# Expert search and dense expert pass: candidates cut from 256 to 50, one-hots on three engines, down projections placed two experts into the next group

## The chip, the cores and the metric

The kernel runs as one program on 1 core of a Trainium2 chip. The metric is device time in microseconds (us). Names of engines: PE is the matrix engine (TensorE; PEld its weight loads), DVE the vector engine, ACT the scalar engine, POOL is GpSimd, SP the engine whose queue issues most DMA transfers. Each engine runs its own instructions strictly in the order in which they stand in its queue.

## The reference, cut to what matters

Two transformer layers (FFN, three attention branches, FFN) are followed by a block with two linear-attention mixers and a product-key expert layer (`_peer`). The change is in that last layer only; all the rest is the same code in both kernels. There are 512 tokens of width 1024, 8 heads, 128 sub-keys per half, 128 x 128 = 16384 experts, each a row of `u_tab` and a row of `v_tab`.

```python
qry = (t @ w_q).reshape(n_tok, 8, 2, 128)
scores = einsum("thpd,hpkd->thpk", qry, sub_keys)          # 128 scores per head and half
s_top, i_top = top_k(scores, 16)
cand = s_top[:, :, 0, :, None] + s_top[:, :, 1, None, :]   # 16 x 16 sums
best, pos = top_k(cand, 16);  idx = take(cand_idx, pos)    # 16 experts per token and head
gate = softmax(best)
act = gelu(einsum("td,thkd->thk", h, u_tab[idx]))
out = einsum("thk,thkd->td", gate * act, v_tab[idx])
```

## The kernel before, in words

**Two ways to one sum.** The first 128 tokens (SPT) take their expert rows by gather: `gathered` issues, on POOL, one indirect DMA for each of 128 (head, k) slots and table (256 in all, plus three steps of run-out), and DVE reduces each (a dot product L1459 for `u`, an accumulation L1466 for `v`). Each call `more(n)` advances that pipeline by n steps, so it is spread over other work; four row buffers (`er`) are in flight. The other 384 tokens (DW) go through ALL 16384 experts densely: in 128 tiles ("experts" in the code, `expert(j)`), activations of 128 experts x 384 tokens are computed on PE, multiplied by a gate matrix that is zero but for the chosen experts, and projected down with `v` in 16 groups of 8 tiles (8 down tiles, m = 0..7, for each group).

**Every matrix product** is `lin`: a 128 x 1024 weight tile is loaded by SP (`raw`, three buffers), split into a high part (`wh`, ACT, L85) and a low part (`wl`, DVE or POOL, L86), and takes 24 matmuls (8 slices x high-high, high-low, low-high). The expert's activation is split the same way into `eh` (ACT, L93) and `el` (DVE, L94).

**Stages of `peer`.** (1) `topk`, first loop, 16 steps (head x half): query product, keys product, and `top16` over 128 scores for four blocks of 128 tokens (five DVE instructions each). (2) `pairs`, for each block of 128 tokens: 256 pair sums on POOL, `top16` over them for 8 heads, then two look-ups (compare on DVE, multiply on POOL over 128 x 2048, reduce on DVE), softmax. The first block's result feeds the gathers; each later block is transposed and *scattered*: for 16 tokens at a time (one tile `stage`, 24 in all) the gate matrix is built by 16 small matmuls of one-hot tiles `lt` (DVE) and `rt` (per token: POOL, DVE or ACT), copied out of PSUM by ACT and written to DRAM (`gate_d`). (3) the dense groups: groups 4 to 15 compute their experts; the activations of groups 0 to 3 (EARLY) were made during stage 2 by `ahead` and are read back from DRAM (`act_d`) at the end.

**What sets the order.** The program is written in one stream; a scheduler assigns each instruction to its engine's queue by that order and by estimated readiness. What stands earlier in the text generally stands earlier in each queue. In the dense part, each group's 8 down tiles come in the text directly behind its 8 experts (L1526 on).

Of the kernel before, what the change touches and what calls it, by code (L numbers as in the profile page):

```python
# [29 lines left out]
TB = 16  # L30
SPT = 128
DW = 512 - SPT
ROUND = 1.5 * 2.0 ** 23
EARLY = 4
# [10 lines left out]
class K:  # L45
# [1423 lines left out]
    def peer(self):  # L1469
# [6 lines left out]
        with tc.tile_pool(name="peer", bufs=1) as mp:  # L1476
            self.mp = mp
            io = mp.tile([128, 144], F, name="io")
            nc.sync.dma_start(io, a["iota"])
            sel = [mp.tile([128, DW], F, name=f"sel{i}") for i in range(5)]  # L1480
# [5 lines left out]
            def more(n):  # L1486
                for _ in range(n):
                    next(rows, None)
# [11 lines left out]
            def ahead(n):  # L1500
                for _, j in zip(range(n), early):
                    nc.sync.dma_start(ad[j], expert(j))

            with tc.tile_pool(name="topk", bufs=1) as tp:
                self.topk(tp, hh, hl, rr, io, sel, gd, ahead, more)
            with tc.tile_pool(name="exp", bufs=1) as ep:
                groups = list(range(EARLY, 16)) + list(range(EARLY))
                for g in groups:
                    wh, wl = [], []
                    last = g == groups[-1]  # L1510
                    for e in range(8):
                        j = g * 8 + e
                        if e == 0:
                            gt = ep.tile([128, DW // TB, 8, TB], F, name="gt", bufs=2)
                            nc.sync.dma_start(gt, gd[:, :, j:j + 8, :])
                        if g < EARLY:
                            act = mp.tile([128, DW], F, name="act", bufs=4)
                            nc.sync.dma_start(act, ad[j])
                        else:
                            act = expert(j)  # L1520
                        av = act.rearrange("p (b t) -> p b t", t=TB)
                        nc.gpsimd.tensor_mul(av, av, gt[:, :, e, :])  # L1522
                        h = ep.tile([128, DW], FR, name="eh", bufs=11)
                        q = ep.tile([128, DW], FR, name="el", bufs=11)
                        self.hilo(act, h, q)
                        wh.append(h)  # L1526
                        wl.append(q)
                        more(0 if last else 1)
                    if g == groups[-2]:
                        more(256)  # L1530
                    for m in range(8):
                        if last and m % 4 == 0:
                            pt = self.bank("pt")
                            for i in range(4):
                                k = m + i
                                nc.tensor.transpose(pt[:, i * 128:i * 128 + 128], self.acc[:, k * 128:k * 128 + 128], self.idn)
                            for i in range(4):
                                x = self.x[m + i][:, 0:SPT]
                                nc.vector.tensor_add(x, pt[:, i * 128:i * 128 + 128], x)
                        ps = self.lin(a["pv"][g, m], 8, wh, wl, cols=slice(0, DW))  # L1540
                        x = self.x[m][:, dn]
                        nc.vector.tensor_add(x, ps[:, 0:DW], x)
                        more(1 if g >= EARLY else 0)
                        if last:
                            self.square(m, m == 7)
                            t = self.xtile()
                            nc.scalar.activation(t, self.x[m], AF.Copy, scale=self.vec[:, 64 + m:65 + m])
                            self.x[m] = t

    def topk(self, sp, hh, hl, rr, io, sel, gd, ahead, more):  # L1550
# [3 lines left out]
        sif = sp.tile([128, 4, 8, 2, 16], F, name="sif")  # L1554
        with tc.tile_pool(name="topk1", bufs=1) as mp:
# [6 lines left out]
            for j in range(16):  # L1562
                ps = self.lin(a["pwq"][j], 8, hh, hl, nc.gpsimd)
                x = mp.tile([128, 512], F, name="qt", bufs=2)
                nc.vector.tensor_mul(x, ps, rr)
                ps = self.bank("sc")
                for t in range(4):
                    c = slice(t * 128, t * 128 + 128)
                    nc.tensor.matmul(ps[:, c], x[:, c], keys[j // 4][:, j % 4], start=True, stop=True)
                s = mp.tile([128, 512], F, name="sc", bufs=2)  # L1570
                nc.scalar.copy(s, ps)
                for t in range(4):
                    w = mp.tile([128, 128], F, name="scr", bufs=2)
                    self.top16(sv[:, t, j // 2, j % 2], si[:, t, j // 2, j % 2], s[:, t * 128:t * 128 + 128], w)
            nc.vector.tensor_copy(sif, si)
        with tc.tile_pool(name="topk2", bufs=1) as mp:
            self.pairs(mp, sv, sif, io, sel, gd, ahead, more)

    def pairs(self, mp, sv, sif, io, sel, gd, ahead, more):
        nc = self.nc  # L1580
        b3, b4 = [128, 8, 16], [128, 8, 16, 16]
        for t in range(4):
            ahead((6, 4, 4, 4)[t])
            s0 = t * 128 - SPT
            cand = mp.tile(b4, F, name="cand", tag="big", bufs=2)
            nc.gpsimd.tensor_tensor(cand, sv[:, t, :, 0].unsqueeze(3).to_broadcast(b4), sv[:, t, :, 1].unsqueeze(2).to_broadcast(b4), op=OP.add)
            best = mp.tile(b3, F, name="best", bufs=1)
            pos = mp.tile(b3, U32, name="pos", bufs=1)
            for h in range(8):
                w = mp.tile([128, 256], F, name="scr2", bufs=2)  # L1590
                self.top16(best[:, h], pos[:, h], cand[:, h].rearrange("p a b -> p (a b)"), w)
            res = [mp.tile(b3, F, name=f"res{i}", bufs=1) for i in range(3)]

            pf = mp.tile(b3, F, name="pf", bufs=1)
            pa = mp.tile(b3, F, name="pa", bufs=1)
            nc.vector.tensor_copy(pf, pos)
            nc.vector.tensor_scalar(pa, pf, -7.5, 0.0625, op0=OP.add, op1=OP.mult)
            nc.vector.tensor_scalar(pa, pa, ROUND, ROUND, op0=OP.add, op1=OP.subtract)
            nc.vector.scalar_tensor_tensor(pf, pa, -16.0, pf, op0=OP.mult, op1=OP.add)
            for x, pf in enumerate((pa, pf)):  # L1600
                e = mp.tile(b4, F, name="eq", tag="big", bufs=2)
                nc.vector.tensor_tensor(e, pf.unsqueeze(3).to_broadcast(b4), io[:, 128:144].unsqueeze(1).unsqueeze(1).to_broadcast(b4), op=OP.is_equal)
                nc.gpsimd.tensor_tensor(e, e, sif[:, t, :, x].unsqueeze(2).to_broadcast(b4), op=OP.mult)
                nc.vector.tensor_reduce(res[x], e, axis=AX.X, op=OP.add)
            g = res[2]
            nc.vector.tensor_tensor(g, best, best[:, :, 0:1].to_broadcast(b3), op=OP.subtract)
            nc.scalar.activation(g, g, AF.Exp)
            z = mp.tile([128, 8], F, name="gz", bufs=1)
            nc.vector.tensor_reduce(z, g, axis=AX.X, op=OP.add)
            nc.vector.reciprocal(z, z)  # L1610
            nc.vector.tensor_tensor(g, g, z.unsqueeze(2).to_broadcast(b3), op=OP.mult)
            if s0 < 0:
                nc.vector.scalar_tensor_tensor(res[0], res[0], 128.0, res[1], op0=OP.mult, op1=OP.add)
                nc.vector.tensor_copy(self.eidx, res[0].rearrange("p h k -> p (h k)"))
                nc.vector.tensor_copy(self.egate, g.rearrange("p h k -> p (h k)"))
                continue
            pt = self.bank("pt")
            for i in range(3):
                nc.tensor.transpose(pt[:, i * 128:i * 128 + 128], res[i].rearrange("p h k -> p (h k)"), self.idn)
            for i in range(3):  # L1620
                nc.vector.tensor_copy(sel[i][:, s0:s0 + 128], pt[:, i * 128:i * 128 + 128])
            nc.vector.tensor_scalar(sel[3][:, s0:s0 + 128], pt[:, 128:256], -1.0, None, op0=OP.mult)
            nc.vector.tensor_scalar(sel[4][:, s0:s0 + 128], pt[:, 256:384], -1.0, None, op0=OP.mult)
            for tb in range(s0 // TB, (s0 + 128) // TB):
                st = mp.tile([128, 128, TB], F, name="stage", bufs=2)
                for t4 in range(TB // 4):
                    ps = self.bank("g")
# [193 lines left out]
```

## Time and profile before

| | |
|---|---|
| three runs | 4918.76, 4922.48, 4921.11 us; median 4921.11 |
| profiled execution | 4921.75 us, span of its instructions 4920.0 us, mean granted clock 0.965 |
| busy over the span | PE 93%, PEld 80%, DVE 65%, ACT 39%, POOL 25% |
| peer layer | from about 3300 us to the end |

The profile is of one execution. Matmuls overlap in the pipeline, so the time of a PE row is longer than its distance to the next row; distances of starts are what counts. "Idle before <- X" says what the engine waited for.

### The profile page before, as it was taken

To read this page: it belongs to the slowest core of one execution; us is meant where nothing else is said; L and a number is where in the kernel's file an instruction comes from. 1 tells how busy PE (TensorE), PEld (TensorE's weight loads), DVE (VectorE), ACT (ScalarE), POOL (GpSimd) and SP (SyncE) were. 2 spreads that over 40 slices of the span, in tenths; PEclk is the share of its full clock that TensorE was granted. 3 is DMA by queue.
4 is the path that set the end of the run, shared out by engine and by line. 5 is a ranking of instruction groups with operands and counts; after the bars stand their busy time and mean duration, and the time that the engine had idled before them with its cause. 6 is when DMAs were issued, how large, how long until landed. Compare 5 with 4: busy or idle time off the path is not lost. (4 is left out here: it accounts for less than half of the span.)

```text
span 4920.0 us, 63316 instructions
## 1 busy us (share of the span) xinstructions
PE 4557.3 (93%) x23070; PEld 3912.1 (80%) x23070; DVE 3198.9 (65%) x6028; ACT 1935.8 (39%) x3343; POOL 1213.8 (25%) x1061
## 2 busy tenths in 40 slices
PE   9999999999999999999999998879677899999987
PEld 7887777788888878777888787767666899999986
DVE  4447877654454478787544578778776666666676
ACT  3235565532232256655322332332466333333322
POOL 0001012200000011132100102322688434434454
PEclk9999999999999999999999998989899999999998
DMA  3234333522333343235333332232354777777785
GB/s 129 94 109 129 93 88 84 176 94 92 98 98 94 102 134 96 79 96 164 98 97 97 110 127 79 73 105 82 124 174 169 248 256 245 240 252 247 238 296 190
DMA packets 276311, 688.30 MB, mean 140 GB/s; under 512 B 32192, under 2 KB 92256, under 8 KB 272928
## 3 DMA queue, kind: packets, MB, share of 16 engines
q1 hardware_dynamic: 239136, 550.02, 35.6%
q0 software_dynamic: 36864, 134.23, 8.2%
q8 instruction: 183, 3.00, 0.2%
q14 instruction: 128, 1.05, 0.1%
HBM read 593.04 MB, written 68.04 MB: 134 GB/s over the span
## 5 line engine op out<-in xcount | busy, mean ns | idle before, releaser
L85 ACT CAST wh<-raw 128x1024 fp32r<-128x1024 f32 (+3 forms) x773 | 766.5, 993 | 1773.7 <-PE bk L107 1130.0
L107 PE MATMUL bk<-hh,wh 128*128 128x512 f32 (+1 forms) x3016 | 1138.3, 377 | 27.4 <-ACT hh L231 9.4
L107 PE MATMUL bk<-hh,wl 128*128 128x512 f32 (+1 forms) x3016 | 1133.6, 376 | 21.8 <-DVE wl L86 20.0
L107 PE MATMUL bk<-hl,wh 128*128 128x512 f32 (+1 forms) x3016 | 1132.8, 376 | 0.5 <-DVE hl L232 0.5
L86 DVE TENSOR_TENSOR wl<-raw,wh 128x1024 fp32r<-128x1024 f32 (+3 forms) x693 | 830.1, 1199 | 159.1 <-ACT wh L85 150.4
L107 PEld LDWEIGHTS bk<-hh,wh 128*128 128x128 f32 x3016 | 574.6, 191 | 109.6 <-issue 16.9
L107 PEld LDWEIGHTS bk<-hh,wl 128*128 128x128 f32 x3016 | 573.9, 190 | 102.8 <-DVE wl L86 23.1
L107 PEld LDWEIGHTS bk<-hl,wh 128*128 128x128 f32 x3016 | 574.4, 190 | 79.4 <-issue 2.7
L107 PE MATMUL bk<-eh,wh 128*128 128x384 f32 x1024 | 366.5, 359 | 71.6 <-ACT eh L93 51.9
L197 POOL TENSOR_TENSOR sq<-sq,sqt 128x512 f32<-128x512 f32 x62 | 104.0, 1677 | 1203.5 <-ACT sqt L193 1184.3
L107 PE MATMUL bk<-el,wh 128*128 128x384 f32 x1024 | 365.9, 358 | 12.2 <-DVE el L94 11.0
L107 PE MATMUL bk<-eh,wl 128*128 128x384 f32 x1024 | 360.2, 354 | 10.6 <-DVE wl L86 10.5
L86 POOL TENSOR_TENSOR wl<-raw,wh 128x1024 fp32r<-128x1024 f32 (+2 forms) x80 | 185.3, 2317 | 587.7 <-ACT wh L85 468.3
L107 PE MATMUL bk<-gh,wh 128*128 128x512 f32 x704 | 274.0, 389 | 0.0
L107 PE MATMUL bk<-gh,wl 128*128 128x512 f32 x704 | 273.9, 389 | 0.0
L107 PE MATMUL bk<-gl,wh 128*128 128x512 f32 x704 | 273.9, 389 | 0.0
L107 PEld LDWEIGHTS bk<-eh,wh 128*128 128x128 f32 x1024 | 207.1, 202 | 82.3 <-ACT eh L93 59.9
L1522 POOL TENSOR_TENSOR act<-act,gt 128x384 f32<-128x384 f32 x128 | 173.5, 1361 | 303.1 <-ACT act L1495 190.0
L256 DVE TENSOR_TENSOR t<-bk,rr 128x512 f32<-128x512 f32 x88 | 60.8, 691 | 269.2 <-PE bk L107 269.2
L107 PEld LDWEIGHTS bk<-el,wh 128*128 128x128 f32 x1024 | 206.3, 201 | 22.2 <-DVE el L94 22.0
L107 PEld LDWEIGHTS bk<-eh,wl 128*128 128x128 f32 x1024 | 206.0, 201 | 13.9 <-DVE wl L86 13.9
L265 DVE SCALAR_TENSOR_TENSOR x<-bk,x 128x512 f32<-128x512 f32 x96 | 66.4, 691 | 231.6 <-PE bk L107 231.6
(703 smaller groups left out, 8827.0 us busy)
## 6 DMA issues: line engine op xcount, KB each, us to landing
raw<-in_wi SPq DMA_DIRECT2D x176, 512.0 KB
raw<-in_pu SPq DMA_DIRECT2D x128, 512.0 KB
raw<-in_pv SPq DMA_DIRECT2D x128, 512.0 KB
raw<-in_wo SPq DMA_DIRECT2D x64, 448.0 KB
raw<-in_mg SPq DMA_DIRECT2D x48, 512.0 KB
gate_d<-stage SPq DMA_DIRECT2D x24, 1024.0 KB
gt<-gate_d SPq DMA_DIRECT2D x16, 1536.0 KB
raw<-in_wo SPq DMA_DIRECT2D x32, 512.0 KB
```

What stands on the lines that cost most here:

```text
L85: self.nc.scalar.copy(wh[:, :n], raw[:, :n])
L86: (eng or self.nc.vector).tensor_sub(wl[:, :n], raw[:, :n], wh[:, :n].bitcast(F))
L107: self.nc.tensor.matmul(ps, x[:, c], y[k], start=(n == 0), stop=(n == 3 * kk - 1))
L197: nc.gpsimd.tensor_add(self.sq, self.sq, t)
L256: nc.vector.tensor_mul(t2, pb, rr)
L265: nc.vector.scalar_tensor_tensor(self.x[m], ps, 0.5, self.x[m], op0=OP.mult, op1=OP.add)
L1522: nc.gpsimd.tensor_mul(av, av, gt[:, :, e, :])
```

## The change

- The candidate sums are cut to those pairs of ranks (a, b) that can be among the best 16, (a+1)(b+1) <= 16: 50 in place of 256 (`RANKS`, `FIRST`, `NC2`). They are built by seven POOL instructions per head for all four token blocks; block 0 is searched inside stage 1. Positions are turned into sub-keys by a comparison with the first position of each row (`found`).
- Generators run the search for block t+1 between the 16-token tiles of the scatter of block t (`run`, `pairs`, `fill`, `scatter`).
- `lt` is built for 8 tokens at once. Of 16 tokens' `rt`, ACT makes 6, POOL 5, DVE 5; before it was ACT 4, DVE 4, POOL 8.
- In stage 1 the query is copied by ACT, and the normalisation is applied by ACT as a scale per token.
- EARLY is 5, and ten of those 40 tiles are computed inside stage 1 (j >= 6), six around the first two searches (their `wl` on POOL), 24 in the scatter (one per tile of 16 tokens). The early groups are put between the others: 5, 6, 0, 7, 8, 1, ... 14, 4, 15.
- The 8 down tiles of a group stand behind the second expert of the next group (`e == 1`), the last group's at the end. `el` is made by POOL in place of DVE. The gather steps are spread anew: 12 in the fill, two per scatter tile, 9 or 8 per group of experts and of down tiles, all before the last down.

```diff
-EARLY = 4
+EARLY = 5
...
+        groups = list(range(EARLY, 16))
+        for i in range(EARLY):
+            groups.insert(3 * i + 2, i)
...
                 h = ep.tile([128, DW], FR, name="eh", bufs=11)
                 q = ep.tile([128, DW], FR, name="el", bufs=11)
-                        self.hilo(act, h, q)
+                nc.scalar.copy(h, act)
+                nc.gpsimd.tensor_sub(q, act, h.bitcast(F))
...
+                more(0 if g < EARLY else 1 + (e == 0))
+                if e == 1 and before:
+                    down(*before, False)
+            before = (g, wh, wl)
+        more(256)
+        down(*before, True)
...
-                nc.vector.tensor_mul(x, ps, rr)
+                nc.scalar.copy(x, ps)
...
+                if j % 2:
+                    for r0, r1 in ((0, 1), (1, 2), (2, 3), (3, 4), (4, 5), (5, 8), (8, 16)):
+                        n, w = r1 - r0, RANKS[r0]
+                        nc.gpsimd.tensor_tensor(cand[:, :, h, FIRST[r0]:FIRST[r1]] ...
+                    pair(0, h)
+                if j >= 6:
+                    ahead(1, nc.gpsimd)
...
+            run(pairs(0), fill(3, 0))
+            run(pairs(1), fill(3, 4))
+            for t in range(1, 4):
+                run(self.scatter(mp, t, io, sel, gd, ahead, more), *[pairs(t + 1)] if t < 3 else [])
...
+        e = mp.tile(b4, F, name="eq", tag="big", bufs=1)
+        nc.vector.tensor_tensor(e, pf..., io[:, 144:160]..., op=OP.is_ge)
+        nc.gpsimd.tensor_tensor(e, e, row..., op=OP.mult)
+        yield
...
+                    if v % 3 == 0:
+                        nc.scalar.activation(rt[:, u], io[:, 0:128], AF.Square, scale=-1.0, bias=sel[1][:, i:i + 1])
+                        nc.scalar.activation(rt[:, u], rt[:, u], AF.Relu, scale=sel[3][:, i:i + 1], bias=g)
+                    else:
+                        (nc.gpsimd if v % 3 == 1 else nc.vector).tensor_scalar(rt[:, u], ...
```

**DVE, search and scatter.** Before, the two look-ups of token block 2 (`eq`, L1602 and L1604) with nothing of a scatter between them:

```order
L1599 SCALAR_TENSOR_TENSOR pf<-pa,pf 128x128
L1602 TENSOR_TENSOR eq<-pa,io 128x2048
L1602 TENSOR_TENSOR eq<-pf,io 128x2048
L1604 TENSOR_REDUCE res_31414<-eq 128x128
L1604 TENSOR_REDUCE res_31415<-eq 128x128
L1609 TENSOR_REDUCE gz<-res_31416 128x8
L1493 TENSOR_TENSOR t_31535<-bk,rr 128x384
```

After, the same search's comparison (L1659) among the one-hots `lt` and `rt` of block 1:

```order
L1708 TENSOR_TENSOR lt<-io,sel_28986 128x1024
L1721 TENSOR_SCALAR rt<-io,sel_28987,sel_28988 128x128 x2
L1657 CAST pf<-pos 128x128
L91 TENSOR_TENSOR wl<-raw,wh 128x1024
L1721 TENSOR_SCALAR rt<-io,sel_28987,sel_28988 128x128
L1659 TENSOR_TENSOR eq<-pf,io 128x2048
L1708 TENSOR_TENSOR lt<-io,sel_28986 128x1024
L1498 TENSOR_TENSOR t_31456<-bk,rr 128x384
```

The look-ups no longer stand alone; DVE has one-hots of another block before and behind each.

**DVE, dense part.** Before, one expert of a group (`t` takes its sum from PSUM, `el` needs ACT's `eh`, L1459 is a gather step), and the next expert's `t`:

```order
L1493 TENSOR_TENSOR t_34958<-bk,rr 128x384
L86 TENSOR_TENSOR wl<-raw,wh 128x1024
L94 TENSOR_TENSOR el<-act,eh 128x384
L1459 ISA er,dot<-er,ht 128x1024
L1459 ISA dot 128x1
L1493 TENSOR_TENSOR t_35001<-bk,rr 128x384
```

After, the place between two groups (`x` adds a down tile's sum): a down tile of an early group, two experts of the next group, then the down tiles go on with the following group's.

```order
L1533 TENSOR_TENSOR x<-bk,x 128x384
L1471 SCALAR_TENSOR_TENSOR acc<-er,ew,acc 128x1024
L91 TENSOR_TENSOR wl<-raw,wh 128x1024
L1498 TENSOR_TENSOR t_36463<-bk,rr 128x384
L1471 SCALAR_TENSOR_TENSOR acc<-er,ew,acc 128x1024
L91 TENSOR_TENSOR wl<-raw,wh 128x1024
L1471 SCALAR_TENSOR_TENSOR acc<-er,ew,acc 128x1024
L1498 TENSOR_TENSOR t_36509<-bk,rr 128x384
L1471 SCALAR_TENSOR_TENSOR acc<-er,ew,acc 128x1024
```

`el` is gone from this queue, so that nothing in it waits for `eh`; experts and down tiles alternate in runs of 2, 6 or 8.

**POOL, dense part.** Before, experts at a group's end and the gathers of its down tiles:

```order
L1522 TENSOR_TENSOR act<-act,gt 128x384
L1452 DMA er<-in_pur,eidx 128x1024
L1452 DMA er<-in_pvr,eidx 128x1024 x4
L1452 DMA er<-in_pur,eidx 128x1024 x4
L1522 TENSOR_TENSOR act<-act,gt 128x384
```

After, the end of group 6, which the early group 0 follows:

```order
L1555 TENSOR_TENSOR act<-act,gt 128x384
L1559 TENSOR_TENSOR el<-act,eh 128x384
L1457 DMA er<-in_pur,eidx 128x1024
L1555 TENSOR_TENSOR act<-act,gt 128x384 x3
L1559 TENSOR_TENSOR el<-act,eh 128x384 x2
L1457 DMA er<-in_pur,eidx 128x1024 x2
L1559 TENSOR_TENSOR el<-act,eh 128x384
```

Each expert has a second POOL operation, `el`, that waits for ACT's `eh`; at this place the gate products of group 0's first two tiles stand ahead of the `el` of group 6's last one.

## Rows read from the trace of the kernel before

**Rows 1.** Stretches: us, busy of PE, PEld, DVE, ACT, POOL, clock, DMA share, GB/s

```profile
3423.00:3519.00 96.00, 66.99 (x325) 63.03 (x324) 80.96 (x219) 27.62 (x36) 35.61 (x10) 0.84 0.29 88
3519.00:3596.00 77.00, 59.88 (x368) 51.56 (x366) 56.69 (x140) 59.81 (x106) 75.60 (x70) 0.98 0.55 190
3596.00:3623.00 27.00, 17.61 (x74) 15.99 (x74) 20.26 (x35) 8.74 (x13) 16.19 (x6) 0.81 0.35 127
3818.00:3860.00 42.00, 34.26 (x176) 32.62 (x175) 29.98 (x33) 14.31 (x24) 18.79 (x17) 0.88 0.86 270
3860.00:4612.00 752.00, 701.31 (x3833) 688.65 (x3832) 501.07 (x664) 246.60 (x341) 306.90 (x240) 0.96 0.75 246
4690.00:4903.00 213.00, 182.44 (x945) 173.32 (x943) 160.88 (x196) 61.14 (x88) 109.76 (x84) 0.90 0.74 251
```

**Rows 2.** Dense part, DVE in order of time, 4268 to 4312 us

```profile
4272.16 0.56 DVE L1493 TENSOR_TENSOR t<-bk,rr 128x384 f32<-128x384 f32 x1 [1.35 <-PE bk L107]
4275.75 0.56 DVE L94 TENSOR_TENSOR el<-act,eh 128x384 fp32r<-128x384 f32 x1 [1.45 <-ACT eh L93]
...
4306.93 0.55 DVE L1493 TENSOR_TENSOR t<-bk,rr 128x384 f32<-128x384 f32 x1
```

**Rows 3.** PE in order of time at the start of a group's down tiles

```profile
4303.18 0.34 PE L107 MATMUL bk<-eh,wh 128*128 128x384 f32 x1
4303.35 0.34 PE L107 MATMUL bk<-el,wh 128*128 128x384 f32 x1
...
4306.15 0.34 PE L107 MATMUL bk<-eh,wl 128*128 128x384 f32 x1
4310.06 0.69 PE L107 MATMUL bk<-eh,wh 128*128 128x384 f32 x1 [3.57 <-ACT eh L93]
...
4311.45 0.53 PE L107 MATMUL bk<-eh,wh 128*128 128x384 f32 x1
4311.77 0.53 PE L107 MATMUL bk<-el,wh 128*128 128x384 f32 x1
```

**Rows 4.** ACT's copies of the scores, one per step of stage 1

```profile
L1571 ACT COPY sc<-sc x16: 575/587/588, 3315.1 to 3422.9; 128x512 f32<-128x512 f32 x16
```

**Rows 5.** Groups by line, stage 1 (3315 to 3423): busy, mean ns, idle before

```profile
L1418 DVE MAX8 sv<-scr 128x8 f32<-128x128 f32 x60 | 16.8, 280 | 0.5
L1569 PE MATMUL sc<-keys,qt 128*128 128x128 f32 x120 | 17.0, 285 | 8.8 <-DVE qt L1565 7.2 <-issue 1.7
```

**Rows 6.** The same view, scatter of all three blocks (3519 to 3818)

```profile
L1641 POOL TENSOR_SCALAR rt<-io,sel,sel 128x128 f32<-128x128 f32 x191 | 211.6, 1115 | 9.4 <-DVE sel L1622 8.2 <-issue 0.3
L1644 ACT COPY stage<-g 128x512 f32<-128x512 f32 x96 | 101.0, 1052 | 56.2 <-PE g L1643 56.1
L1639 ACT ACTIVATE rt<-rt,sel,sel 128x128 f32<-128x128 f32 x96 | 46.8, 490 | 2.1
L1638 ACT ACTIVATE rt<-io,sel 128x128 f32<-128x128 f32 x94 | 36.7, 393 | 0.0
L1641 DVE TENSOR_SCALAR rt<-io,sel,sel 128x128 f32<-128x128 f32 x95 | 32.8, 345 | 0.0
L86 DVE TENSOR_TENSOR wl<-raw,wh 128x1024 fp32r<-128x1024 f32 x22 | 27.2, 1243 | 0.0
L1603 POOL TENSOR_TENSOR eq<-eq,sif 128x2048 f32<-128x2048 f32 x4 | 22.1, 5542 | 25.0 <-DVE eq L1602 25.0
L85 ACT CAST wh<-raw 128x1024 fp32r<-128x1024 f32 x21 | 22.0, 1045 | 34.2 <-PE bk L107 24.8 <-DVE gz L1610 9.4
L1459 DVE CUSTOM_DVE_ANT_0 er<-er,ht 128x1024 f32<-128x1024 f32 x13 | 17.0, 1307 | 3.7 <-DMA er<-in_pur,eidx 3.7
L1604 DVE TENSOR_REDUCE res<-eq 128x128 f32<-128x2048 f32 x4 | 9.1, 2286 | 13.3 <-POOL eq L1603 13.3
```

**Rows 7.** The same view, ten dense groups (3860 to 4612)

```profile
L1522 POOL TENSOR_TENSOR act<-act,gt 128x384 f32<-128x384 f32 x80 | 109.0, 1362 | 231.2 <-ACT act L1495 170.3 <-issue 60.8
L1452 POOL DMA_INDIRECT er<-in_pur,eidx x80 | 106.3, 1329 | 110.0 <-DVE acc L1466 84.0 <-DMA raw<-in_pu 19.9 <-issue 4.1
```

More of the change, by code (lines that the diff above doesn't have):

```diff
@@ L32 @@
 DW = 512 - SPT
+RANKS = [16 // (a + 1) for a in range(16)]
+FIRST = [sum(RANKS[:a]) for a in range(17)]
+NC2 = FIRST[16]
 ROUND = 1.5 * 2.0 ** 23
-EARLY = 4
+EARLY = 5
 EPS = 1e-6
@@ L1477, in peer @@
             self.mp = mp
-            io = mp.tile([128, 144], F, name="io")
+            io = mp.tile([128, 176], F, name="io")
             nc.sync.dma_start(io, a["iota"])
-            sel = [mp.tile([128, DW], F, name=f"sel{i}") for i in range(5)]
+            sel = [mp.tile([128, DW], F, name=f"sel{i}") for i in range(4)]
             ht = self.by_token(rc)
@@ L1498, in peer, with ahead @@
             early = iter(range(EARLY * 8))
-            def ahead(n):
+            def ahead(n, eng=None):
                 for _, j in zip(range(n), early):
-                    nc.sync.dma_start(ad[j], expert(j))
+                    nc.sync.dma_start(ad[j], expert(j, eng))
             with tc.tile_pool(name="topk", bufs=1) as tp:
-                self.topk(tp, hh, hl, rr, io, sel, gd, ahead, more)
+                self.topk(tp, hh, hl, rc, io, sel, gd, ahead, more)
             with tc.tile_pool(name="exp", bufs=1) as ep:
[L1507 to L1524, printed above, removed]
-                        self.hilo(act, h, q)
[L1526 to L1548, printed above, removed]
@@ L1552, in topk @@
+    def topk(self, sp, hh, hl, rc, io, sel, gd, ahead, more):
         nc, tc, a = self.nc, self.tc, self.a
@@ new lines, in topk, with run, pairs, fill @@
+        with tc.tile_pool(name="topk2", bufs=1) as mp:
+            def run(*gens):
+                gens = list(gens)
+                while gens:
+                    for g in list(gens):
+                        if next(g, gens) is gens:
+                            gens.remove(g)
+            def pairs(t):
+                if t:
+                    for h in range(8):
+                        pair(t, h)
+                        if h % 2:
+                            yield
+                for _ in self.found(mp, t, best[:, t], pos[:, t], sif[:, t, :, 1], row[:, t], io, sel):
+                    yield
+            def fill(n, m):
+                for _ in range(n):
+                    ahead(1, nc.gpsimd)
+                    more(m)
+                    yield
+            run(pairs(0), fill(3, 0))
+            run(pairs(1), fill(3, 4))
+            for t in range(1, 4):
+                run(self.scatter(mp, t, io, sel, gd, ahead, more), *[pairs(t + 1)] if t < 3 else [])
@@ L1648, in pairs @@
-        ahead(32)
+        res = [mp.tile(b3, F, name=f"res{i}", bufs=1) for i in range(3)]
+        pf = mp.tile(b3, F, name="pf", bufs=1)
+        pa = mp.tile(b3, F, name="pa", bufs=1)
+        nc.vector.tensor_copy(pf, pos)
+        e = mp.tile(b4, F, name="eq", tag="big", bufs=1)
+        nc.vector.tensor_tensor(e, pf.unsqueeze(3).to_broadcast(b4), io[:, 144:160].unsqueeze(1).unsqueeze(1).to_broadcast(b4), op=OP.is_ge)
+        nc.gpsimd.tensor_tensor(e, e, row.unsqueeze(2).to_broadcast(b4), op=OP.mult)
```

192 lines of the change are left out of this document (123 added, 69 removed).

## The prediction

> **What bounds the kernel now.** I read the profile in this order: the busy shares by stretch, then the order in time of DVE and PE where PE falls idle in the dense part, then the groups by line of the three stages. The stretches [rows 1] are the first search (3423 to 3519), eight of the scatter's 24 blocks (3519 to 3596), a gap between two token blocks (3596 to 3623), and the dense part, which begins at 3818. PE is the engine to feed: the tail is 17 us, all else up to 4903 is products. One product of 24 matmuls costs PE 24 x 0.173 = 4.16 us, from the distance of starts where it runs undisturbed (4303.18 to 4303.35) [rows 3].
>
> In the dense part 94 experts are left at 3818 (128 less 32 early ones less the two that the order has done by then) and 128 down tiles: 222 x 4.16 = 923.5 us, but it takes 4903 - 3818 = 1085. So 161 us are lost. Ten groups in the middle take 752 us for 160 products, which need 666: 8.6 us lost for each. The 42 us at the start hold about seven products (29), 13 lost; the 213 us at the end, with four early groups in a row, hold 39 (162), 51 lost [rows 1].
>
> The loss stands at a group's turn. DVE's queue holds, per expert, `t`, `wl`, `el` and a gather step, and `el` waits for ACT's `eh` (1.45 us idle); seven experts take 4306.93 - 4272.16 = 34.8 us, 4.97 each [rows 2]. That is 0.81 more than PE needs, so DVE is 5.6 us behind at the eighth, and the down tiles, which need that expert at once, leave PE idle for 3.57 us at one wait, after which starts are 0.32 apart instead of 0.17, the lower of the clock's two levels (1.2 for 2.4 GHz) [rows 3].
>
> In the scatter POOL is busy 75.6 of 77 us: 9.6 per block of 16 tokens, and in the gaps 16.2 of 27 while PE stands at 17.6 [rows 1]. The stage takes 299 us: 24 x 9.6 = 231, and 68 for two searches with no scatter beside them. POOL's multiply in a look-up (5.5 us) waits 25 us in four for DVE's comparison, and DVE's reduce 13 for POOL [rows 6].
>
> **The change, step by step.** The sum is against the profiled execution, 4921.75 us (0.6 above the median of the runs), whose span is 4920.0.
>
> *Stage 1.* A step takes (3422.9 - 3315.1)/15 = 7.19 us [rows 4], of which PE is idle 8.8/15 = 0.6 for the query that DVE copies [rows 5]; ACT's copy removes about half. Six steps at 6.9 and ten with an expert (6.6 + 4.16 = 10.8) give 149: last scores at about 3464 instead of 3423. Ten products for 41 us: neither gain nor loss. DVE has, per step, four `top16` (1.2 each: five instructions of about 0.25, MAX8 being 0.28 for 128 [rows 5]), half of a block-0 pair search and `t`: about 6, hidden under 10.8. Without that cover the ten steps would each cost a few tenths.
>
> *First search.* The 96 us [rows 1] shrink to what follows the last score. The look-ups pass serially through one buffer: compare about 2.3, multiply 5.54, reduce 2.29 [rows 6], 1 of hand-over: 11.1, four times is 44. Finishing scans 9; eight gathers that POOL's new order puts ahead of the third multiply, at 1.33 [rows 7], about 11; transposes 5. The first block starts near 3464 + 70 = 3534 (bounds 3515, if the searches overlap, and 3550). Six early experts, 25 us of PE, lie under these 70; PE waits for the rest of them.
>
> *Scatter block.* From rows 6 and 7: POOL 5 x 1.115, two gather issues of 1.33 and an eighth of two multiplies: 9.6. ACT 6 x (0.393 + 0.490) + 4 x 1.052 + 1.045 for `wh`: 10.6. DVE `lt` 2 x 1.24 (no row has this form; `wl` is as wide; 0.6 if it ran at twice that rate, 2.5 at half), 5 x 0.345, `wl` 1.24, `t` 0.55 [rows 2], two dot products of 1.31: 8.6, and for the next search (2 x 2.3 + 2 x 2.29 + 8 scans of 0.9 + 2)/8 = 2.3: 10.9. PE has an expert and 16 small products, about 7, and waits. Three engines at nearly one length must meet in each block, so below 9.6 is excluded; if they take turns it is 13 or more. I take 11.0 for sixteen blocks, near the longest engine as POOL's 9.6 was in before, and 10.5 for the last eight, without search: 260 us (bounds 238 and 312). The scatter ends near 3794, with 40 experts done instead of 34.
>
> *Dense part.* 88 experts and 128 down tiles remain: 216 x 4.16 = 898.6. Without `el`, DVE has per expert 4.97 - 1.45 - 0.56 = 2.96: no longer late. POOL has `act` and `el`, 1.36 each (the nearest row is `act`, same shape), about 0.6 of waiting for `eh`, and one issue of 1.33 [rows 7]: 4.65, which is 0.5 above PE's 4.16, so now POOL falls behind, by 4 us over eight experts. At the turns: after groups 5, 7, 9, 11, 13 two experts (8.3 us) cover it, 1 us lost each: 5. The early groups 0 to 4 have no experts; two of the next group stand before their down tiles, while POOL makes 16 products and `el`, 22 us, and gathers in 41: 4 each, 20. Groups 6, 8, 10, 12, 14 are followed by an early group, so nothing of PE's stands between their eighth expert and their down tiles, and the order shows POOL's products for the early group ahead of the eighth `el`: 9 each, as now: 45. The last group 6, the start 12 (13 now). Losses 88 instead of 161 (bounds 48 and 160). Spreading the gathers puts their end ahead of the last down tile; the order shows no gather step behind it, so the tail stays 17.
>
> Sum: 3794 + 898.6 + 88 + 17 = 4797.6 of span, and 1.75 around it: **4799 us**, 122 less. Of these, 24 are the earlier end of the scatter, 25 the six experts more, 73 the turns.
>
> **The shared port.** DVE is busy 501 of 752 us in the dense part [rows 1], mostly with operations on two tiles, and POOL's `act` still averages 1.36 [rows 7] against 0.56 for DVE's `el` of the same shape [rows 2]. The Trainium skill (SBUF — State Buffer, "Who interferes with whom") says that a DVE instruction with two SBUF inputs and a GpSimd instruction that reads SBUF contend for a port pair that is held exclusively. The trace of before neither shows such a wait nor excludes that 1.36 holds one. By that rule 256 POOL operations where 128 stood would meet it; what it would cost is the slower rival.
>
> **The rivals.**
> - *B, scatter blocks of 13 us.* ACT, DVE and POOL are each near 10 to 11 and hand tiles to one another through few buffers. For: POOL already waits for DVE's `eq` [rows 6]. Against: before, POOL kept 75.6 of 77 us [rows 1]. 24 x 13 = 312, 52 more: 4851.
> - *C, the turns stall as before, behind POOL instead of DVE; the two experts between do not help.* Eleven turns at 8.6, five early at 11, start 12: 160 lost instead of 88: 4871. For: 4.65 is over 4.16. Against: 8.3 us of cover exceeds the lag of 4. In part this is the change not doing what it says, since six of sixteen groups' down tiles have no expert between anyway.
> - *D, everything overlaps better.* Blocks of 10 (20 less) and 48 lost (40 less): 4740.
> - *A, POOL sets the pace of the dense part.* It has 256 products and subtractions and 199 gather issues: 128 x (2.72 + 0.6) + 199 x 1.33 = 690 us against 987 forecast. If each of the 455 is held 1.0 us behind DVE's operations, 1145: end 3794 + 1145 + 17, 4958 us, slower. It binds from 0.65 us per operation, and is slower than before from (1109 - 690)/455 = 0.92. Against: DVE was as busy and 1.36 came out [rows 1, 7].
>
> **How the numbers follow.** Forecast 0.46, B 0.18, C 0.12, D 0.12, A 0.08, and B with C together 0.04: 4923, no change. Less than 0.2%, 10 us, cannot be told from none by such runs. Faster is all but A and the last: 0.88; same 0.04; slower 0.08. The likeliest case's own range is 4770 to 4830. For 8 in 10 it must take in B and C and most of D, and leaves out A, B with C, and half of D: 4745 to 4890.
>
> **What the profile after would show.** The first block of the scatter near 3534; blocks 10.5 to 11 apart, with ACT and DVE as busy as POOL; the end near 3794. In the dense part no wait of DVE for `eh`, POOL's `el` at about 1.36, PE's idle before down tiles of 1 us where two experts stand between, and about 9 with a low clock after groups 6, 8, 10, 12, 14. Gathers that end before the last down tile. It is wrong if `el` on POOL takes well over 2 us, if blocks are beyond 12, or if PE waits for gate or weight loads in the early groups, which now stand between the others.

## The result, and the profile after

The changed kernel takes 4833.0 us (median of four runs, 4826.6 to 4839.2) against 4921.8 for the kernel before: a ratio of 0.9821, interval [0.9803, 0.9838]. That is 89 us (1.8%) less where the prediction had 122; it lies in the stated range and 3 us above the likeliest case's own (4770 to 4830). The profiled execution is the fastest of the four, 4826.6 us with a span of 4824.8.

The same view as [rows 1], now in five stretches: stage 1, what follows its last score, the scatter with searches beside it, the scatter of the last token block, the dense part.

```profile
3307.00:3446.00 139.00, 139.00 (x721) 121.50 (x720) 93.31 (x617) 59.43 (x121) 67.12 (x73) 1.00 0.35 104
3446.00:3529.00 83.00, 51.25 (x235) 47.91 (x234) 73.27 (x176) 22.25 (x36) 48.66 (x29) 0.79 0.48 154
3529.00:3712.00 183.00, 137.00 (x779) 124.23 (x778) 145.82 (x258) 142.86 (x281) 166.55 (x110) 0.86 0.64 218
3729.00:3816.00 87.00, 72.16 (x441) 66.75 (x440) 64.61 (x96) 71.89 (x140) 80.06 (x55) 0.95 0.73 251
3815.00:4807.00 992.00, 938.76 (x5191) 930.11 (x5190) 709.90 (x755) 333.28 (x468) 615.08 (x459) 0.97 0.74 251
```

Stage 1 is all PE, at full clock. POOL is still the busiest engine of the scatter (166.6 of 183, 80.1 of 87), and in the dense part its share has grown by half: 615 of 992 us (62%), where it was 307 of 752 (41%) [rows 1]. Against the working of the prediction:

| step | forecast | measured |
|---|---|---|
| last score | 3464 | 3445 |
| first block of the scatter | 3534, 70 later | 3529, 84 later |
| length of the scatter, to PE's last product of it | 260 | 285 |
| dense part, 216 products of 4.16 | 898.6 | 898.6 |
| lost there | 88 | 94 |
| behind the last down tile | 17 | 17.4 |
| span | 4797.6 | 4824.8 |

Against the kernel before, the scatter ends about 3 us earlier (3814.5; its last product was at 3817.1), six more experts are done by then (25 us), and the dense part loses 94 us instead of 161 (67): together 95, and the spans differ by 95.2.

**The scatter.** Groups by line over it, as in [rows 6] (busy, mean ns, idle before):

```profile
L1721 POOL TENSOR_SCALAR rt<-io,sel,sel 128x128 f32<-128x128 f32 x119 | 182.6, 1539 | 16.1 <-issue 5.7 <-ACT wh L90 5.0 <-ACT rt L1719 1.8
L1725 ACT COPY stage<-g 128x512 f32<-128x512 f32 x96 | 100.5, 1053 | 52.3 <-PE g L1724 51.4 <-issue 0.4
L1708 DVE TENSOR_TENSOR lt<-io,sel 128x1024 f32<-128x1024 f32 x47 | 58.1, 1236 | 0.0
L1721 DVE TENSOR_SCALAR rt<-io,sel,sel 128x128 f32<-128x128 f32 x118 | 46.1, 420 | 55.0 <-POOL rt L1721 23.5 <-issue 18.3 <-ACT rt L1718 4.0
L1668 DVE TENSOR_TENSOR res<-res,gz 128x128 f32<-128x128 f32 x2 | 0.7, 352 | 0.0
```

`lt` costs 1.24 us, as estimated, but POOL's `rt` 1.54 where 1.115 was taken from [rows 6]. Five of them are 2.1 us more per block. Blocks follow each other at 12.1 us while a search runs and at 11.2 without one (forecast 11.0 and 10.5); the step to the last token block, 18 us, is in neither mean. With it the first sixteen blocks take 199 us and the last eight 86, where 176 and 84 were forecast.

What stretches them is easiest to see in the second search, where operations stand alone. POOL in order of time:

```profile
3460.03 4.58 POOL L1660 TENSOR_TENSOR eq<-eq,row 128x2048 f32<-128x2048 f32 x1 [5.56 <-DVE eq L1659]
...
3515.80 4.51 POOL L1678 TENSOR_TENSOR eq<-eq,sif 128x2048 f32<-128x2048 f32 x1 [5.89 <-DVE eq L1677]
```

and DVE at the same two moments:

```profile
3460.49 4.27 DVE L1668 TENSOR_TENSOR res<-res,gz 128x128 f32<-128x128 f32 x1
...
3517.01 4.38 DVE L91 TENSOR_TENSOR wl<-raw,wh 128x1024 fp32r<-128x1024 f32 x1
```

A product of two small tiles that takes 0.35 us in the scatter's mean row takes 4.27, and `wl` 4.38 instead of 1.24: each ends only behind POOL's long multiply, `res` 0.15 us after it and `wl` 1.08. In the scatter it goes the other way too. Sorted by what ran beside them ("on two tiles" means that both inputs are tiles in SBUF), POOL's 118 `rt` of the scatter take 0.80 us where DVE runs nothing on two tiles, and about 2.0 where it does for half of their time or more; before the change the same classes had 0.78 and 1.41, beside `lt` tiles half as wide. The Trainium skill (SBUF — State Buffer, "Who interferes with whom") states this: a DVE instruction with two inputs in SBUF and a GpSimd instruction that reads SBUF cannot run together, and the second waits out the first. The traces agree, by the times just given.

**The dense part.** What PE lost at its turns, from the distances of PE's starts in order of time: all over 0.173 us in the gaps, and the starts at the lower clock (about 0.31 apart) behind them. Turns with two experts between are called covered below, those of the second line straight.

| turn | forecast | measured |
|---|---|---|
| five with two experts between (behind 5, 7, 9, 11, 13) | 5 | 34 |
| five straight behind the eighth expert (6, 8, 10, 12, 14) | 45 | 32 |
| five of early groups | 20 | 6 |
| last group, start, and the remainder | 6, 12, 0 | 5, 8, 9 |

So the sum came out near (88 and 94), but not by its terms. The covered turns should have cost 1 us each, and they cost most. PE at such a turn, in the second down tile of group 11:

```profile
4424.30 0.34 PE L112 MATMUL bk<-el,wh 128*128 128x384 f32 x1
4428.98 0.69 PE L112 MATMUL bk<-eh,wl 128*128 128x384 f32 x1 [4.34 <-DVE wl L91]
4429.47 0.52 PE L112 MATMUL bk<-eh,wh 128*128 128x384 f32 x1
4429.78 0.52 PE L112 MATMUL bk<-el,wh 128*128 128x384 f32 x1
```

Not the group's `eh` or `el` is late, as in [rows 3], but the weight's low part. DVE in order of time says why:

```profile
4418.61 0.55 DVE L1498 TENSOR_TENSOR t<-bk,rr 128x384 f32<-128x384 f32 x1
4426.56 1.23 DVE L1464 CUSTOM_DVE_ANT_0 er<-er,ht 128x1024 f32<-128x1024 f32 x1 [7.40 <-DMA er<-in_pur,eidx]
4427.71 0.08 DVE L1464 DVE_READ_ACCUMULATOR2_ANT dot<- 128x1 f32 x1
4427.71 1.22 DVE L91 TENSOR_TENSOR wl<-raw,wh 128x1024 fp32r<-128x1024 f32 x1
```

DVE stood 7.4 us at a gather step, with `wl` behind it. The row it waited for goes into the buffer that this step freed on DVE:

```profile
4403.84 1.96 DVE L1471 SCALAR_TENSOR_TENSOR acc<-er,ew,acc 128x1024 f32<-128x1024 f32 x1
```

which ends at 4405.80; POOL asked for the row 9.4 us later, at 4415.24, behind the products of two experts:

```profile
4408.43 1.72 POOL L1559 TENSOR_TENSOR el<-act,eh 128x384 fp32r<-128x384 f32 x1 [0.63 <-ACT eh L1558]
4410.30 1.79 POOL L1457 DMA_INDIRECT er<-in_pur,eidx  x1
4412.10 1.02 POOL L1555 TENSOR_TENSOR act<-act,gt 128x384 f32<-128x384 f32 x1
4413.75 1.34 POOL L1559 TENSOR_TENSOR el<-act,eh 128x384 fp32r<-128x384 f32 x1 [0.63 <-ACT eh L1558]
4415.24 0.98 POOL L1457 DMA_INDIRECT er<-in_pur,eidx  x1
```

The n-th issue on POOL belongs to the n-th step on DVE and uses the buffer of step n - 4. Over the dense part the issue comes 6.9 us (median) after its buffer is free; before the change it came 0.3 after. So POOL's lag, which the prediction saw, reaches PE by way of the gathers and DVE.

The late issue is not all of it. The rows then took 11.3 us, and at the same time 1.5 MB of gates are loaded for the next group, issued at 4413.15. At all five covered turns the row that DVE waits for was asked for 8 to 11 us after its buffer was free and 2 us behind such a load, and came 9.4 to 11.9 us after it was asked for; at the step of 4718.1, with no load near, a waited-for row came after 5.4. What the load adds by itself was not tried.

DVE did not become lighter either. Its groups over the dense part (the same three with `el` back on DVE stand in that experiment):

```profile
L91 DVE TENSOR_TENSOR wl<-raw,wh 128x1024 fp32r<-128x1024 f32 x209 | 296.2, 1417 | 31.0 <-ACT wh L90 30.8
L1471 DVE SCALAR_TENSOR_TENSOR acc<-er,ew,acc 128x1024 f32<-128x1024 f32 x100 | 156.3, 1563 | 22.8 <-DMA er<-in_pvr,eidx 22.7
L1464 DVE CUSTOM_DVE_ANT_0 er<-er,ht 128x1024 f32<-128x1024 f32 x93 | 143.9, 1548 | 38.5 <-DMA er<-in_pur,eidx 38.4
```

### The profile page after: what moved, and what is told of

It reads as the page before. It is cut to its first block, busy times and chain, and to the rows that moved or that the text cites. A ratio compares the mean times of both kernels' runs of the same rounds, so it can differ in the third digit from the quotient of the medians.

```text
span 4824.8 us, 63302 instructions
## 1 busy us (share of the span) xinstructions
PE 4528.9 (94%) x23070; PEld 3914.1 (81%) x23070; DVE 3171.7 (66%) x5836; ACT 1976.6 (41%) x3515; POOL 1412.6 (29%) x1185
## 5 line engine op out<-in xcount | busy, mean ns | idle before, releaser
L91 DVE TENSOR_TENSOR wl<-raw,wh 128x1024 fp32r<-128x1024 f32 (+3 forms) x677 | 842.7, 1246 | 144.3 <-ACT wh L90 137.7
L91 POOL TENSOR_TENSOR wl<-raw,wh 128x1024 fp32r<-128x1024 f32 (+2 forms) x96 | 224.3, 2338 | 569.9 <-ACT wh L90 447.3
L112 PE MATMUL bk<-eh,wh 128*128 128x384 f32 x1024 | 356.4, 348 | 14.7 <-ACT eh L1558 14.7
L1464 DVE CUSTOM_DVE_ANT_0 er<-er,ht 128x1024 f32<-128x1024 f32 x128 | 187.6, 1467 | 48.1 <-DMA er<-in_pur,eidx 48.1
L1471 DVE SCALAR_TENSOR_TENSOR acc<-er,ew,acc 128x1024 f32<-128x1024 f32 x128 | 201.3, 1573 | 23.5 <-DMA er<-in_pvr,eidx 23.5
```

The lines of the kernel that those rows point to most:

```text
L91: (eng or self.nc.vector).tensor_sub(wl[:, :n], raw[:, :n], wh[:, :n].bitcast(F))
L112: self.nc.tensor.matmul(ps, x[:, c], y[k], start=(n == 0), stop=(n == 3 * kk - 1))
L1464: order(nc.vector.tensor_tensor_reduce(out=r, in0=r, in1=ht, scale=1.0, scalar=0.0, op0=OP.mult, op1=OP.add, accum_out=dots[b][:, i:i + 1]))
L1471: order(nc.vector.scalar_tensor_tensor(acc, r, ws[b][:, i:i + 1], acc, op0=OP.mult, op1=OP.add))
```

## The experiments

All are edits of the changed kernel (4833.0 us), each timed beside the kernel before; the ratios are to that. An interval is about 0.2% to either side, 10 us, and smaller differences between two kernels are not told apart. The last score falls anywhere from 3438 to 3449 in kernels with the same stage 1, so stages are compared by their own lengths: the scatter takes 285 to 292 us in the five kernels that leave it as it is.

**One-hots: two fewer on POOL.**

```diff
-(nc.gpsimd if v % 3 == 1 else nc.vector).tensor_scalar(rt[:, u], ...
+(nc.gpsimd if v % 6 == 1 else nc.vector).tensor_scalar(rt[:, u], ...
```

> Of each 16 one-hots `rt`, POOL makes 3 in place of 5 and DVE 7 in place of 5. Theory (in the changed kernel POOL's `rt` took 1.54 us instead of 1.12, because it runs beside DVE operations on two tiles; so POOL is the longest engine of a block): POOL's work per block falls from 11.5 to 8.4 us, ACT's 10.6 is then the longest, blocks shrink from 11.9 to about 10.8 on the mean, the scatter from 285 to about 260 us, the time to about 4810. Rival (three engines in turn through two `rt` buffers, no one engine's length decides): blocks stay at 12.1 with and 11.2 without search, time within 8 us of 4833. A second rival (DVE, 10.9 us by the forecast's sum, is the true limit): blocks grow by 0.7 us, time about 4850.

4810.6 us, ratio 0.9769 [0.9753, 0.9786]. The scatter takes 268 us, 17 less where 25 were expected. Its groups by line:

```profile
L1721 POOL TENSOR_SCALAR rt<-io,sel,sel 128x128 f32<-128x128 f32 x72 | 122.9, 1708 | 50.7 <-ACT wh L90 11.5 <-issue 10.3 <-ACT rt L1719 9.2
L1721 DVE TENSOR_SCALAR rt<-io,sel,sel 128x128 f32<-128x128 f32 x168 | 69.8, 469 | 23.9 <-issue 13.7 <-ACT rt L1719 4.4 <-POOL rt L1721 2.9
```

POOL now has idle time ahead of its `rt` and DVE hardly waits for it (2.9 us, 23.5 in the changed kernel). POOL was the limit, and another follows closely. Two of its `rt` cost 3.1 us or more per block, the same two on DVE about 0.9.

**Half of `lt` left out.**

```diff
-                if t4 % 2 == 0:
+                if t4 == 0:
                     i = tb * TB + t4 * 4
                     lt = mp.tile(bc, F, name="lt", bufs=2)
```

> Leaves out every second one-hot tile `lt` of the scatter (the first eight tokens' tile is used for sixteen), so DVE has 1.24 us less of operations on two tiles per block; POOL's instructions are the same. Theory (POOL's `rt` is held while DVE works on two tiles: 0.78 us beside none, about 2 us beside one): mean of POOL's `rt` falls from 1.54 to about 1.3 us, each block by about 1.2 us, the scatter by 25 to 30 us, time about 4806. Rival (POOL's `rt` is long for another reason, as its own queue or its scalar operands): `rt` stays at 1.5 and the blocks at 11.2 to 12.1.

The tile of the first eight tokens serves for all sixteen. 4805.3 us, ratio 0.9771 [0.9750, 0.9791]; the scatter takes 261 us. POOL's work is untouched, and its `rt` is shorter:

```profile
L1721 POOL TENSOR_SCALAR rt<-io,sel,sel 128x128 f32<-128x128 f32 x117 | 153.6, 1317 | 15.2 <-POOL rt L1721 3.5 <-DVE lt L1708 2.5 <-issue 2.1
```

1.317 as expected (1.3); where the scatter is left as it is, the mean lies between 1.54 and 1.64. Less work of DVE on two tiles makes POOL faster: the mechanism is shown. That the width of `lt` matters, and not only how much of DVE's time goes to two tiles, is not shown by it. Whether handing tiles on through two `rt` buffers costs anything besides was not tried.

**The search behind the scatter in place of between its tiles.**

```diff
-                run(self.scatter(...), *[pairs(t + 1)] if t < 3 else [])
+                run(self.scatter(...))
+                if t < 3:
+                    run(pairs(t + 1))
```

> The search for a token block runs after the scatter of the block before it, not between its tiles. If the interleaving is what the scatter stage won: 24 blocks at the 11.2 us that blocks without a search have (269), and two gaps of about 27 and 34 as before the change: 330 us instead of 285, time about 4877. Rival (the search costs as much between the blocks as alone): within 10 us of 4833.

4844.5 us, ratio 0.9851 [0.9830, 0.9872]: 11 us, not 44. The scatter takes 306 us, 21 more (15 to 21, by the other kernels). The gap at its first search, and the blocks behind it:

```profile
3609.00:3646.00 37.00, 29.62 (x163) 27.81 (x162) 36.55 (x50) 19.35 (x34) 17.20 (x9) 0.94 0.59 193
3646.00:3717.00 71.00, 50.86 (x295) 43.29 (x295) 53.70 (x118) 58.57 (x121) 65.89 (x50) 0.90 0.64 218
```

A gap still adds 27 us, but blocks without a search follow at about 10.6 us instead of 12.1, and PE is busy 29.6 of 37 us in the gap: three more experts are done by the scatter's end (85 left, not 88), which is 12.5 us of the 21. Both theories were wrong in size: the interleaving hides two gaps of 27 us, and gives most of that back, about 24 us in longer blocks and 12.5 in experts that the gaps had held. With the search out of the scatter POOL's `rt` averages 1.40 us instead of 1.54: the search's own work on two tiles is part of what stretches them.

**Down tiles straight behind their own group.**

```diff
-                if e == 1 and before:
-                    down(*before, False)
-            before = (g, wh, wl)
-        more(256)
-        down(*before, True)
+            if g == groups[-1]:
+                more(256)
+            down(g, wh, wl, g == groups[-1])
```

> The down tiles go directly behind their own group's eighth expert, as before the change; all else as in the changed kernel. The forecast's step (two experts between save 8 us at each of five turns): about 40 us slower, 4873. Theory after seeing the trace (with two experts between, PE loses 6.8 us at these turns all the same, to DVE's low weight part `wl` that stands behind a gather step; without them 6.4): within 10 us of 4833.

4884.3 us, ratio 0.9920 [0.9903, 0.9937]: 51 slower. The theory formed after the trace (no difference) falls, and the forecast's step (40) stands. The dense part loses 150 us, 55 more: every turn now waits, those of the early groups too. PE at the turn behind group 10 (the same place, with other names, as [rows 3]):

```profile
4331.14 0.44 PE L112 MATMUL bk<-eh,wh 128*128 128x384 f32 x1 [2.00 <-ACT eh L1558]
4332.54 0.45 PE L112 MATMUL bk<-el,wh 128*128 128x384 f32 x1 [0.96 <-POOL el L1559]
4332.82 0.34 PE L112 MATMUL bk<-eh,wl 128*128 128x384 f32 x1
4336.04 0.69 PE L112 MATMUL bk<-eh,wh 128*128 128x384 f32 x1 [2.88 <-ACT eh L1558]
```

**`el` on DVE again.**

```diff
-                nc.gpsimd.tensor_sub(q, act, h.bitcast(F))
+                nc.vector.tensor_sub(q, act, h.bitcast(F))
```

> `el` is made by DVE again, the down tiles stay two experts behind. Forecast's step (el on DVE makes DVE late by 0.81 us per expert; turns without cover lose 8.6 instead of 6.4, covered ones are covered): about 11 us slower, 4844, or more if the experts themselves fall behind. Rival (the covered turns lose their 6.8 us because POOL, made late by `el`, issues the gathers late): five covered turns are freed, about 20 to 30 us faster, 4808.

4826.3 us, ratio 0.9805 [0.9788, 0.9821]: not told apart from the changed kernel. DVE waits 126 us for `eh` again, and yet the dense part loses 85 us instead of 94. The gather steps' waits for their rows, 61 us in the changed kernel (38.4 and 22.7), are gone, and POOL issues 0.7 us after a buffer is free:

```profile
L91 DVE TENSOR_TENSOR wl<-raw,wh 128x1024 fp32r<-128x1024 f32 x210 | 262.4, 1250 | 23.9 <-ACT wh L90 23.6 <-issue 0.2
L1471 DVE SCALAR_TENSOR_TENSOR acc<-er,ew,acc 128x1024 f32<-128x1024 f32 x101 | 133.1, 1318 | 1.3 <-issue 1.1
L1464 DVE CUSTOM_DVE_ANT_0 er<-er,ht 128x1024 f32<-128x1024 f32 x96 | 123.3, 1286 | 1.3 <-DMA er<-in_pur,eidx 1.3
L1559 DVE TENSOR_TENSOR el<-act,eh 128x384 fp32r<-128x384 f32 x125 | 84.3, 684 | 131.0 <-ACT eh L1558 125.7 <-issue 5.3
```

The covered turns lose 17 us together instead of 34, so the rival is right in part, and the straight ones 44 instead of 32. Without `el` on POOL, DVE's other operations are shorter: `wl` 1.25 us instead of 1.42, the accumulation 1.32 instead of 1.56, the dot product 1.29 instead of 1.55. Over the counts shown that is 84 us, as much as the 84 that `el` takes here. So DVE is busy 697 of 983 us with `el` and 710 of 992 without it: handing `el` to POOL took nothing off DVE. With the down tiles two experts behind, moving `el` off DVE is worth nothing.

**Gather steps away from the turns.**

```diff
-                more(0 if g < EARLY else 1 + (e == 0))
+                more(0 if g < EARLY or e < 2 else 1)
...
-                more(0 if last or g < EARLY and m % 2 else 1)
+                more(0 if last else m % 2 == 0 or g < 3 and m == 7 if g < EARLY else 1 + (m % 3 == 1))
```

> The three gather steps of a group's first two experts are moved among its down tiles; the number of steps is the same. Theory (at a covered turn DVE stands 2 to 7 us in a gather step whose rows POOL asked for late, and the second down tile's `wl` is queued behind it): the idle of PE before `eh,wl` products at the five covered turns falls from 34 us to under 10, about 25 us faster, 4808. Rival (these turns lose because POOL's `el` or the weight loads are late, whatever the gathers do): the same idle, within 8 us of 4833.

4812.4 us, ratio 0.9778 [0.9761, 0.9794]: 21 faster. Groups of PE over the dense part, of the changed kernel first:

```profile
L112 PE MATMUL bk<-eh,wl 128*128 128x384 f32 x1010 | 351.5, 348 | 27.8 <-DVE wl L91 27.8
L112 PE MATMUL bk<-eh,wh 128*128 128x384 f32 x1011 | 352.0, 348 | 14.7 <-ACT eh L1558 14.7
```

and with the steps moved:

```profile
L112 PE MATMUL bk<-eh,wl 128*128 128x384 f32 x1024 | 354.3, 346 | 7.9 <-DVE wl L91 7.7
L112 PE MATMUL bk<-eh,wh 128*128 128x384 f32 x1024 | 354.2, 346 | 21.5 <-ACT eh L1558 15.3 <-ACT wh L90 6.2
```

PE's wait for `wl` falls by 20 us with the same work on every engine, and issues come 3.0 us after their buffers are free; four of the five covered turns now lose 2 us or less, near the forecast's 1 (the first, behind group 5, still 7), and the dense part 74.

**Early groups at the end.**

```diff
-            groups.insert(3 * i + 2, i)
+            groups.append(i)
```

> The five early groups stand behind group 15, in a row, instead of between the others. If their place matters as in the kernel before, where four in a row lost 50 us: five turns with no expert of PE to cover POOL's work, about 6 us each beyond the present 1.2, so 25 us slower, 4858. Rival (POOL's products for an early group fit into the 33 us of down tiles ahead of it, wherever it stands, and four turns that have no cover now get one): within 10 us of 4833.

4847.1 us, ratio 0.9857 [0.9835, 0.9878]: 14 slower, where 25 were expected. The dense part loses 110 us instead of 94, 26 of them behind the first of the last 48 down tiles.

**One-hots and gather steps together.**

> POOL makes 3 of 16 `rt`, and the three gather steps of a group's first two experts stand among its down tiles. The two gains lie in different stages, the scatter and the dense part, so they should add: 22 and 21 us, 4790. Rival (what the scatter wins is given back at the start of the dense part, or the gathers then run past the last down tile): 4805 or more.

4789.8 us, ratio 0.9729 [0.9707, 0.9751]. They add: 43 us below the changed kernel, 22 and 21 by themselves.

**Cover for every turn, on top of that.**

```diff
-            early = iter(range(EARLY * 8))
+            early = iter([j for j in range(EARLY * 8) if j % 8 > 1])
...
-                if j >= 6:
-                    ahead(1, nc.gpsimd)
...
-                if g < EARLY:
+                if g < EARLY and e > 1:
```

> On top of the two edits together (4790): the first two experts of each early group are computed in their place in the dense part and not ahead, so that every group's down tiles have two experts between; stage 1 then computes none of the experts. Theory (what a turn loses is the lack of PE work between the last expert and its down tiles): the five turns with about 9 to 10 us lost go to 1, 45 us won for ten products of 4.16 more in the dense part, and stage 1 is 25 to 30 us shorter: about 4760. Rival (stage 1 is held by DVE's searches without its experts, or POOL, with ten products more, is late everywhere): 4785 or more.

4797.1 us, ratio 0.9751 [0.9727, 0.9775]: no gain over 4790. The first block does come 39 us earlier (3494), but ten more products (42 us) stand in the dense part and its loss stays, 81 us. Its groups of PE:

```profile
L112 PE MATMUL bk<-eh,wl 128*128 128x384 f32 x980 | 339.9, 347 | 29.5 <-DVE wl L91 29.4
L112 PE MATMUL bk<-eh,wh 128*128 128x384 f32 x980 | 338.3, 345 | 13.4 <-ACT wh L90 12.0 <-ACT eh L1558 1.1
```

The wait for `eh` is gone (1.1), as the theory had it, and the wait for `wl` is back (29.4). In that kernel DVE stands at a gather step again, inside a group's down tiles:

```profile
4656.40 0.55 DVE L1533 TENSOR_TENSOR x<-bk,x 128x384 f32<-128x384 f32 x1
4663.73 1.23 DVE L1464 CUSTOM_DVE_ANT_0 er<-er,ht 128x1024 f32<-128x1024 f32 x1 [6.78 <-DMA er<-in_pur,eidx]
```

The stall was turned into another; a turn's cover alone is not what decides.

**No gathers in the second search, on top of the two edits.**

```diff
-            run(pairs(1), fill(3, 4))
+            run(pairs(1), fill(3, 0))
...
-                more(... else 1 + (m % 3 == 1))
+                more(... else 1 + (m % 3 == 1 or m == 6))
```

> On top of the two edits together (4790): the twelve gather steps in the second search are moved to the dense part, ten of them among the down tiles. Theory (the first block is late because eight gather issues stand on POOL ahead of the third look-up's multiply, and eight dot products on DVE ahead of its sum): the multiply follows its comparison at once, the first block starts 15 to 20 us earlier, about 3513 to 3518, and the time falls by 10 to 18 us, 4776, since PE had idle time there. Rival (the searches' own serial chain sets the start): the start moves by less than 5 us, the time by none, or up by some us for the steps in the dense part.

4775.7 us, ratio 0.9707 [0.9687, 0.9728]: 14 less, or 11 by the ratios, whose intervals overlap; and the fastest kernel here, 142 us below the kernel before and 57 below the changed one. What is clear of the spread is the start: the first block comes at 3509, 67 us behind the last score (83 to 85 in every kernel with the steps in the search). The dense part, which got the twelve steps, loses 90 us where the two edits alone lost 78. POOL at the third and fourth multiplies of this kernel, with one gather issue left in the search; in the changed kernel they began at 3496.0 and 3515.8:

```profile
3478.00 1.98 POOL L1457 DMA_INDIRECT er<-in_pur,eidx  x1 [3.25 <-DVE best L1420]
3483.26 4.54 POOL L1660 TENSOR_TENSOR eq<-eq,row 128x2048 f32<-128x2048 f32 x1 [3.28 <-DVE eq L1659]
3495.25 4.53 POOL L1678 TENSOR_TENSOR eq<-eq,sif 128x2048 f32<-128x2048 f32 x1 [7.45 <-DVE eq L1677]
```

DVE in the changed kernel, the first of four dot products in a row and the sum behind them; the multiply that this sum needs had ended at 3500.5, 6.0 us before:

```profile
3501.93 1.21 DVE L1464 CUSTOM_DVE_ANT_0 er<-er,ht 128x1024 f32<-128x1024 f32 x1
...
3506.51 2.27 DVE L1670 TENSOR_REDUCE res<-eq 128x128 f32<-128x2048 f32 x1
```

**Cover and the free search together.**

> Both of these together. If the gains lie in different stages they add: 4790 less 30 less 14, about 4746. If the steps moved to the dense part meet the ten products there: 4760 or more.

4789.2 us, ratio 0.9736 [0.9716, 0.9755]: 13 above the same kernel without the cover, so no gain here either.

## Why the prediction was right, and where its terms were not

- *Stage 1, no gain and no loss from ten experts there: right, and its end better by luck.* Scores end 19 us before the forecast: the first comes at 3307 and not 3315 [rows 4], which the prediction did not see, and it counted sixteen steps where fifteen intervals lie between the first score and the last. These 19 us hid half of what the next two terms were short, 14 and 25; without them the time would have been about 4852, outside the likeliest case's own range. PE is busy in all 139 us. Taking the experts out moved the first block by 39 us for 42 us of products.
- *First search, 70 us: 84.* The gathers' price was put at 11 us for POOL's issues ahead of the third multiply. Moving them away brought 17 us back, 84 to 67: DVE's dot products in the same queue (the rows at 3501.93 and 3506.51) and its waits for their rows were left out of the term.
- *Scatter blocks of 11.0 and 10.5: 12.1 and 11.2. This is the term that was mis-sized, 25 us.* POOL's `rt` was priced by its mean before the change, 1.115, and took 1.54, though the same change puts more of DVE's work on two tiles beside it. The prediction held that the trace of before showed no such wait; sorted by what ran beside it, POOL's `rt` showed it there already (0.78 and 1.41). The rule on the shared port was weighed, but against the dense part alone, where it was the slower rival. There it lengthened DVE's operations by as much as `el` had taken, and cost PE little; in the scatter, where POOL was already full, it cost time. Rival B's price (52 us more) was too high, and what the runs show behind the longer blocks is the port and not, as it had it, engines handing tiles on; that reason was not tried by itself.
- *The turns: the sum right, the terms wrong.* "Two experts (8.3 us) cover it, 1 us lost each" failed by 29 us over five turns. The lag of 4.65 against 4.16 was there, and the cover did hide the late `el`; but POOL's lag also made its gather issues late, and DVE's queue had those steps ahead of the second down tile's `wl`. The early groups and the straight turns came out about 14 and 13 us better than put, for no reason that the prediction had: that 94 is near 88 is luck. That placement is what the turns gained is shown (51 us without it); the 73 us forecast for the dense part were 67.
- *`el` off DVE, the step from which the dense argument began, did not matter.* With `el` back on DVE the time cannot be told from the changed kernel's: the lag moves between DVE and POOL, and the 0.56 us that the term took off DVE per expert came back as longer `wl` and gather steps.
- *Rival C, no help from the two experts: no, but near at the covered turns.* They lost 6.7 us each, nearer to its 8.6 than to the forecast's 1; the dense part as a whole lost 94, not 160.
- *Rival A, POOL as the pace of the dense part: no.* `act` and `el` took 1.23 and 1.26 us there, below the 1.36 of [rows 7], and POOL is busy 62%.

What stays open: whether the straight turns can be freed without a new wait of DVE (the one attempt did not do it), what the gate loads add at the covered ones, and what the cut to 50 candidates, the query's copy on ACT and the wider `lt` are worth by themselves, which no run tried.

## What to carry to other kernels

A duration taken from a trace holds only beside the neighbours it had: when a change hands work from POOL to DVE or gives DVE more operations on two tiles, price POOL's instructions again by the rows that ran beside such operations, and give POOL fewer of them than stand-alone durations suggest. Work handed from DVE to POOL is priced the same way: what DVE keeps may grow by as much as it gave away, as `el` showed. When a consumer is placed later to cover a late engine, read what else that engine issues late, and whose queue holds that ahead of the consumer's other inputs. And if a sum comes out while its terms are unverified, check each turn by itself: here moving three gather steps per group gave 21 us that the near-right sum had hidden.

## What the runs showed of the hardware that was not expected

A small DVE product on two tiles (128 x 128) waits as long as a large one: 4.27 us beside POOL's multiply of 4.58, 0.35 alone. POOL's record of an instruction includes such waits, so that "busy 166.6 of 183 us" was in part waiting: with half of `lt` gone the same 120 `rt` averaged 1.317 us instead of 1.539, 27 us less in sum. And a gather issue on POOL takes 0.98 us or 1.79, as the rows at 4415.24 and 4410.30 show. Beside the longer one DVE runs a `wl`, which itself had waited for the `el` that ends at 4410.15; the issue ends 0.86 us behind it:

```profile
4409.34 1.89 DVE L91 TENSOR_TENSOR wl<-raw,wh 128x1024 fp32r<-128x1024 f32 x1
```

Over the dense part such an issue averages 1.48 us with `el` on POOL and 1.27 with `el` on DVE.
